# Eight small moves in the order of a three-block transformer kernel: taps, operands, banks, yields

## The chip, the cores and the metric

The kernel runs on one core of one Trainium2 chip. The metric is the device time of one execution in microseconds; less is better. Everything is fp32 at the edges.

## What is computed

Three residual blocks follow each other on one sequence of 1024 tokens of width 1024. Block 1 mixes an mLSTM branch (a causal convolution of width 4, gates, a chunkwise recurrence), a differential causal attention and a memory attention. Block 2 mixes a banded attention and a spatial gating unit and has a gated feed-forward part. Block 3 has 16 meta tokens, an LRU branch, a convolution branch of width 31 and a feed-forward part of width 4096. Between the blocks stand RMS norms. Cut to what matters here:

```python
def reference(x, mem, ...):
    x = first_block(x, mem, norm_g, w_in, conv_w, ...)
    x = second_block(x, norm_mix_2, w_in_2, ..., w_ffn_in_2, w_ffn_out_2, norm_final_2)
    return third_block(x, meta_tokens_3, norm_mix_g_3, w_in_3, ..., cc_conv_w_3, ..., norm_final_g_3)

def rmsnorm(x, g):
    return x * lax.rsqrt(jnp.mean(x * x, axis=-1, keepdims=True) + EPS) * g

# block 1, differential attention
pd = p[:, :, 0] - lam * p[:, :, 1]
outs.append(jnp.einsum('bhqk,bhkd->bhqd', pd, v[:, :, :hi]))
# block 2, feed-forward
g, up = jnp.split(hn @ w_ffn_in[l], 2, axis=-1)
h = h + (jax.nn.silu(g) * up) @ w_ffn_out[l]
# block 3, feed-forward
m = rmsnorm_3(h, norm_mlp_g[l]) @ w_mlp_up[l]
h = h + jnp.square(jax.nn.relu(m)) @ w_mlp_down[l]
```

## The kernel before

**Exact products from two halves.** TensorE multiplies fp32r operands. Every fp32 operand is split into a rounded high half and the rest: `split` (line 170) lets ACT cast the high half and DVE subtract it (line 175). `mm3` (lines 161 to 168) then makes three matmuls: high by high, high by low, low by high. Weights come by DMA on SP's queue (line 65) and are split whole by ACT (line 76) and DVE (line 77) into tiles `wsplit`; four of these rotate. A dense product is tiled into 128x512 output tiles, each 8 slices of the inner dimension by 3 matmuls.

**Banks.** PSUM is held as two banks `mm`, two score tiles `sc` of two banks each, and two tiles `tp` for transposes and sums. Where the order of work needs several outputs at once (the first product behind each norm), `gemm_fm` with `group=2` walks over the inner dimension for two outputs at a time and takes its banks from `banks` (line 147): two `mm`, then the four halves of the score tiles, and so on.

**The order of work.** The program is written as Python generators. A main stream issues products unit by unit, and `tick()` after each unit steps side generators (norms, attention steps, convolutions, loads), each up to its next `yield`. What is issued first comes first in a list scheduler, which then orders each engine's queue by it and by readiness. `high_priority` pulls the evictions of PSUM ahead, and `behind(...)` holds an instruction behind given others.

**Norms and seams.** At the end of a block the last product's eviction adds to the residual (L1341 in block 2, L1735 in block 3, L781 in block 1), ACT squares and POOL adds the squares (`square_sum`, L206). `norm_gen` (line 463) sums them by matmul, takes a reciprocal root on DVE in small steps (`rsqrt`, lines 189 to 194), broadcasts it by a transpose (`row_of`, L226), and makes eight split tiles `xs[k, h]` for each half h of the tokens. Where two norms follow each other (the seams 1 to 2 and 2 to 3) a second factor `fg` is multiplied in (line 485).

**Block products.** Two wide feed-forward products are made in `block_gemm` (line 366) with seven products of sums in place of eight: `block_tokens` (line 339) makes the token sums T1 to T4 by DVE and splits them; `operand(j)` (line 378) makes the weight sums `ssum` on POOL (L385, L386, L388, L390) and splits them. Six operands are made ahead of the matmul (L413). `block_up` (line 1435) makes the product of the first four weights while `block_tokens` runs at its side; then `block_gemm` starts and makes its first operands.

**Other places.** `mlstm_gen` (line 880): per channel tile four DVE steps of the convolution (L889, L891), then two tanh on ACT (L895); L702 is an ACT eviction of a unit beside it. `diff_out` (line 1180): for head and pair of query blocks, transposes, splits and value matmuls with a yield after each. `block3` starts with `conv_taps(0)` (line 1707): a DMA of the taps on POOL's queue, a cast on ACT (L1862) and a subtract on DVE. `conv_w` (line 1866) makes convolution matrices, one half on POOL, one on DVE (L1872), in the `wsplit` tiles of the weights; one matrix serves eight steps of three matmuls (L1890). `final` (line 1796): the last product in column pieces of 512 and 256, with the add on DVE (L1810), squares on ACT, sums on POOL (L206), and the sums' matmul (L214).

Of the kernel before, what the change touches and what calls it, by code (L numbers as in the profile page):

```python
# [95 lines left out]
class Kern:  # L96
# [4 lines left out]
    def __init__(self, tc, A):  # L101
        self.tc, self.nc, self.A = tc, tc.nc, A
        self.sides = []


# [41 lines left out]
    def banks(self):  # L147

        while True:
            yield self.mm()  # L150
            yield self.mm()
            for _ in (0, 1):
                sc = self.sc()
                yield sc[:, :512]
                yield sc[:, 512:]

    def tp(self):
# [71 lines left out]
    def gemm_fm(self, n_units, src, evict, halves=(0, 1), N=512, lag=1, gate=None, post=None, wait=None, ahead=True,  # L229
# [4 lines left out]
        if group:  # L234
# [5 lines left out]
            for h in halves:  # L240
                for g in range(0, lag, group):
# [9 lines left out]
                    for k in range(8):  # L251
# [6 lines left out]
                        if k % 2 or len(us) > 2:  # L258
                            yield
                    late += [(u, h, pss[u - g]) for u in us]  # L260
                    if group > 3 or post is not None or (h == halves[-1] and us[-1] == lag - 1):
                        with self.tc.high_priority(offset=PRIO_E):
                            ends()
# [102 lines left out]
    def block_gemm(self, n, B, page, out):  # L366
# [11 lines left out]
        def operand(j):  # L378
# [16 lines left out]
            return w, o  # L395
        ps, x12 = {}, {}
        for j, (p, i) in enumerate(seq):
            for q in range(len(ready), min(j + 6, len(seq))):
# [64 lines left out]
    def norm_gen(self, h, u, g, xs, acc, acc2=None, fg=None, r_d=None, lead=1, stay=False, tight=None):  # L463
# [19 lines left out]
        if fg is not None:  # L483
            gg = self.nsm.tile([128, 8], F32, name="ngg")
            nc.vector.tensor_mul(gg, fg, g)
        else:
            gg = g
# [392 lines left out]
    def mlstm_gen(self):  # L880
# [4 lines left out]
        for k in range(4):  # L885
            a = self.page(name="xcv")
            x = xm[k]
            cw = lambda t: v("conv_w", t * 4 + k)
            nc.vector.tensor_scalar(a, x, cw(3), v("conv_b", k), op0=OP.mult, op1=OP.add)  # L889
            for s in (1, 2, 3):  # L890
                nc.vector.scalar_tensor_tensor(a[:, s:], x[:, :1024 - s], cw(3 - s), a[:, s:], op0=OP.mult, op1=OP.add)  # L891
            for h in (0, 1):
                t = self.half_tmp("ct")
                s = slice(h * 512, h * 512 + 512)
                nc.scalar.activation(t, a[:, s], AF.Tanh)  # L895
                nc.vector.scalar_tensor_tensor(a[:, s], t, 1.0, a[:, s], op0=OP.add, op1=OP.mult)
            xcv.append(a)
            yield
# [281 lines left out]
    def diff_out(self, vd):  # L1180

        nc = self.nc
        for hd in range(4):
            od = self.xpage(name="od")
            for i in range(4):
# [4 lines left out]
                for c in range(i + 1):  # L1190
# [8 lines left out]
                    for k in (0, 1):  # L1199
# [3 lines left out]
                        self.mm3(acc[:, o:o + n], vd[hd, kt // 4], (kt % 4) * 128, 128, t, k * 256, n, kt == 0, last)  # L1203
                    if c < i:
                        yield
# [44 lines left out]
    def block2(self, xs, gens):  # L1250
# [148 lines left out]
        def out(i, block, t, ps):  # L1399
# [7 lines left out]
            else:  # L1407
                self.ends = nc.vector.tensor_mul(t, t, ps),
                store(2 + i, 0, t)
        self.block_up(uu, xs, gens, B, dict.fromkeys(("T1", "T2", "T3", "T4"), self.split_page), ev_up)  # L1410
        for _ in self.block_gemm(20, B, page, out):
            self.tick()
# [21 lines left out]

    def block_up(self, u, xs, gens, B, pages, ev):

        def blocks():
            while any(g in self.sides for g in gens):
                yield
            yield from self.block_tokens(u, xs, gens, B, pages)  # L1440
        tg = self.spawn(blocks())
        for _ in self.gemm_fm(4, lambda k, h: xs[k, h], ev, lag=4, wait=xs, ahead=False, group=2):
            self.tick()
        self.finish(tg, *gens)
# [160 lines left out]
    def block3(self, u2, xs, gens):  # L1605
# [100 lines left out]
        self.hl, self.co = {}, {}  # L1706
        self.conv_taps(0)
        self.spawn(self.conv_in())
# [12 lines left out]
        for i, q in enumerate(SEQ_3):  # L1721
            n = len(" ".join(SEQ_3[:i + 1]).split()) - u0
            for _ in self.gemm_fm(n, src, lambda u, h, ps: ev(u + u0, h, ps),
                                  post=lambda u: (lambda j, w: meta(j + u0, w)) if units[u + u0][0] != "l" else None):
                self.tick()
# [47 lines left out]
        xsp = lambda: self.xpage((128, 2, 512), F32R, "sp")  # L1773
        self.block_up(uu, xs, gens, B, dict(T1=self.split_page, T2=xsp, T3=xsp, T4=self.split_page), ev_up)
        first = [self.xpage, self.xpage]

        def page(shape=(128, 1024), name="pg"):
            return (first.pop() if first else self.page)(shape, F32, name)
        for _ in self.block_gemm(14, B, page, out):
            self.tick()  # L1780
# [15 lines left out]
    def final(self, u3, src):  # L1796
# [4 lines left out]
        for o, n in FINAL:  # L1801
            acc = self.page((128, n), name="acc")
            h, off = divmod(o, 512)
            for m in range(8):
# [4 lines left out]
                with self.tc.high_priority(offset=PRIO_E):  # L1809
                    nc.vector.tensor_add(u, u, ps[:, :n])  # L1810
                    self.square_sum(acc, u, m == 0, eng=nc.gpsimd)
                self.tick()
# [53 lines left out]
    def conv_w(self, i):  # L1866

        for j in range(i, min(i + 2, 9)):
            if j not in self.cw:
                w = self.cw[j] = self.ws.tile([128, 2, 1024], F32R, name="wsplit")  # L1870
                for a, eng in enumerate((self.nc.gpsimd, self.nc.vector)):
                    eng.tensor_tensor(w[:, a, :].rearrange("p (n c) -> p n c", c=32),  # L1872
                                      self.cmask[:, None, :].to_broadcast([128, 32, 32]),
                                      self.taps[a][:, j * 32:j * 32 + 32, None].to_broadcast([128, 32, 32]), op=OP.mult)
        return self.cw.pop(i)

# [344 lines left out]
```

## Time and profile before

| | us |
|---|---|
| median of 3 runs | 3361.07 (3359.77 to 3361.33) |
| the profiled execution's own time | 3369.31 |
| its span in the trace | 3367.6 |
| TensorE busy in the span | 3267.9 |
| VectorE, ScalarE, GpSimd busy | 1914.6, 1167.1, 473.1 |
| mean granted clock of TensorE | 0.987 |

The page counts an engine as busy while an instruction of it runs. A row of a timeline gives the start, the duration, engine and line, the tile written and the tiles read, the shape, how many instructions it stands for, and in brackets how long the engine was idle before it and what it waited for. A row of the windows gives a stretch's length, PE's busy time with its count of matmuls, the granted clock as a share of full speed, the busy share of the DMA engines and GB/s.

### The profile page before, as it was taken

The numbers are of one execution on the slowest core, as the hardware profiler recorded it, in microseconds if no ns is written. First come the engines' busy times: TensorE is split into PE (matmuls) and PEld (weight loads), VectorE is DVE, ScalarE is ACT, GpSimd is POOL, SyncE is SP. The second block draws the span as 40 slices with busy tenths as digits, with TensorE's granted clock in tenths as the row PEclk, the third lists the DMA queues.
The fourth block names the chain that finished last, engine by engine and source line by source line (L and its number), as shares of the span: only waits on it lengthen the run. The fifth ranks groups of instructions, "written<-read, shape, count | busy, mean of one in ns | idle before, by whom it ended". The sixth has DMA issues, their size and how long they took to land.

```text
span 3367.6 us, 41745 instructions
## 1 busy us (share of the span) xinstructions
PE 3267.9 (97%) x16039; PEld 2668.9 (79%) x16039; DVE 1914.6 (57%) x3627; ACT 1167.1 (35%) x2112; POOL 473.1 (14%) x445
## 2 busy tenths in 40 slices
PE   7999999999999999999999999999999999999998
PEld 5788877777777988887788887887878788888887
DVE  6555556665665554346755556445558865554444
ACT  4222344432454442213433333134453443332211
POOL 0000000001300000012223221031202222220002
PEclk9999999999999999999999999999999999999999
DMA  3323211221211144323122235122111333362211
GB/s 116 129 100 125 90 57 38 80 109 63 80 48 41 65 142 163 128 97 128 58 86 82 86 134 190 58 84 70 50 57 66 104 113 105 118 253 96 67 51 57
DMA packets 128632, 318.53 MB, mean 95 GB/s; under 512 B 16304, under 2 KB 34864, under 8 KB 128432
## 3 DMA queue, kind: packets, MB, share of 16 engines
q1 hardware_dynamic: 103392, 234.01, 20.3%
q0 software_dynamic: 21440, 76.51, 6.5%
q10 hardware_dynamic: 3600, 5.34, 0.5%
q8 instruction: 126, 2.06, 0.3%
q14 instruction: 74, 0.61, 0.1%
HBM read 232.90 MB, written 82.90 MB: 94 GB/s over the span
## 4 chain that ended last, share of the span: by engine, by line
PE 82%; DVE 8%; issue 5%; ACT 2%; DMA 2%; POOL 1%; ACTq 0%; POOLq 0%; DVEq 0%; SPq 0%
PE mm L166 16%; PE mm L167 16%; PE mm L168 16%; PE mm L413 10%; PE sc L413 8%; DVE sp L175 1%; PE mm L1890 1%; PE sc L1158 1%; PE sc L166 1%; PE sc L1468 1%; PE sc L167 1%; PE sc L168 1%; DVE wsplit L77 1%; PE tp L166 1%; PE tp L167 1%
## 5 line engine op out<-in xcount | busy, mean ns | idle before, releaser
L166 PE MATMUL mm<-sp,wsplit 128*128 128x512 f32 (+1 forms) x2720 | 1085.5, 400 | 19.1 <-DVE ur L1341 6.7
L167 PE MATMUL mm<-sp,wsplit 128*128 128x512 f32 (+1 forms) x2720 | 1068.5, 393 | 2.8 <-DVE sp L1983 2.5
L168 PE MATMUL mm<-sp,wsplit 128*128 128x512 f32 (+1 forms) x2720 | 1066.9, 392 | 0.0
L166 PEld LDWEIGHTS mm<-sp,wsplit 128*128 128x128 f32 x2720 | 516.9, 190 | 129.5 <-DVE ur L1341 7.8
L167 PEld LDWEIGHTS mm<-sp,wsplit 128*128 128x128 f32 x2720 | 517.4, 190 | 103.6 <-DVE sp L1983 4.1
L168 PEld LDWEIGHTS mm<-sp,wsplit 128*128 128x128 f32 x2720 | 516.5, 190 | 104.8 <-issue 0.8
L413 PE MATMUL mm<-sp,wsplit 128*128 128x512 f32 x1632 | 390.0, 391 | 3.9 <-ACT hd L1761 1.8
L76 ACT CAST wsplit<-wraw 128x1024 fp32r<-128x1024 f32 x196 | 205.5, 1049 | 509.8 <-PE mm L168 475.1
L413 PEld LDWEIGHTS mm<-sp,wsplit 128*128 128x128 f32 x1632 | 305.8, 188 | 71.1 <-DVE scp L430 2.4
L77 DVE TENSOR_TENSOR wsplit<-wraw,wsplit 128x1024 fp32r<-128x1024 f32 x196 | 248.0, 1267 | 164.4 <-ACT wsplit L76 162.8
L413 PE MATMUL sc<-sp,wsplit 128*128 128x512 f32 x1224 | 296.6, 391 | 3.8 <-ACT scp L419 3.0
L413 PEld LDWEIGHTS sc<-sp,wsplit 128*128 128x128 f32 x1224 | 230.6, 189 | 53.7 <-ACT scp L419 3.5
L206 POOL TENSOR_TENSOR acc<-acc,sqt 128x512 f32<-128x512 f32 (+1 forms) x105 | 135.5, 1303 | 471.2 <-ACT sqt L205 382.1
L1735 DVE TENSOR_TENSOR ur<-ur,mm 128x512 f32<-128x512 f32 x112 | 76.9, 686 | 145.3 <-PE mm L168 145.2
L175 DVE TENSOR_TENSOR wsplit<-ssum,wsplit 128x512 fp32r<-128x512 f32 x136 | 101.0, 743 | 93.4 <-ACT wsplit L175 93.3
L1341 DVE SCALAR_TENSOR_TENSOR ur<-mm,ur 128x512 f32<-128x512 f32 x96 | 66.2, 690 | 107.2 <-PE mm L168 107.1
L175 ACT CAST wsplit<-ssum 128x512 fp32r<-128x512 f32 x136 | 82.8, 621 | 108.9 <-POOL ssum L390 35.0
L388 POOL TENSOR_TENSOR ssum<-ssum,wraw 128x512 f32<-128x512 f32 x34 | 51.4, 1512 | 248.8 <-DVE wsplit L175 248.8
L175 ACT CAST wsplit<-wraw 128x512 fp32r<-128x512 f32 x102 | 61.8, 620 | 68.3 <-PE sc L413 47.6
L175 ACT CAST sp<-hraw 128x512 fp32r<-128x512 f32 x108 | 63.3, 620 | 51.9 <-PE mm L168 43.7
L166 PE MATMUL mm<-wsplit,sp 128*128 128x256 f32 x256 | 76.8, 300 | 1.8 <-ACT ot L702 1.8
L175 DVE TENSOR_TENSOR sp<-hraw,sp 128x512 fp32r<-128x512 f32 x108 | 71.1, 686 | 6.6 <-ACT sp L175 6.6
(567 smaller groups left out, 4440.0 us busy)
## 6 DMA issues: line engine op xcount, KB each, us to landing
wraw<-W SPq DMA_DIRECT2D x264, 512.0 KB, 3.7
hraw<-hid_d POOLq DMA_DIRECT2D x54, 512.0 KB, 5.0
hid_d<-scp SPq DMA_DIRECT2D x68, 256.0 KB, 2.0
t_d<-gl SPq DMA_DIRECT2D x32, 256.0 KB, 2.0
u<-x_d POOLq DMA_DIRECT2D x16, 512.0 KB, 6.3
gl<-t_d POOLq DMA_DIRECT2D x32, 256.0 KB, 3.1
u_d<-u SPq DMA_DIRECT2D x32, 256.0 KB, 2.0
ur<-u_d POOLq DMA_DIRECT2D x16, 512.0 KB, 9.3
```

Of the source, the lines that this page charges most:

```text
L76: K.nc.scalar.copy(s[:, 0, :], r)
L77: K.nc.vector.tensor_sub(s[:, 1, :], r, s[:, 0, :].bitcast(F32))
L166: t.matmul(ps, wh, xh, start=first, stop=False)
L167: t.matmul(ps, wh, xl, start=False, stop=False)
L168: t.matmul(ps, wl, xh, start=False, stop=last)
L175: return nc.scalar.copy(hi, src), nc.vector.tensor_sub(lo, src, hi.bitcast(F32))
L206: eng.tensor_add(acc, acc, t[:, :acc.shape[-1]])
L388: nc.gpsimd.tensor_sub(s, s, a11)
L413: nc.tensor.matmul(d, wk[:, c, :], xk[:, e, :], start=new and k == y == 0, stop=k == 3 and y == 2, skip_group_check=not new)
L1158: nc.tensor.matmul(pss[m][:, kb * 512:kb * 512 + w], qt[P, a, qs], kt[P, b, :w], start=i == 0, stop=i == 2 and not diag)
L1341: nc.vector.scalar_tensor_tensor(uu(m, h), ps, 0.5, uu(m, h), op0=OP.mult, op1=OP.add)
L1735: nc.vector.tensor_add(uu(m, h), uu(m, h), ps)
```

## The change

Eight places are edited. (1) `banks` gives the score halves first, then the `mm` banks. (2) `block_gemm` makes its first four operands in front of its loop, with a yield after each two; `block_up` steps it there after T1 and after T2, but not before three groups of its own product are issued. (3) `norm_gen` yields once more in the seams. (4) `mlstm_gen` yields between convolution and tanh. (5) `diff_out` leaves out the three yields of the last head's last pair. (6) the first `conv_taps` is held behind the last split of the norm that was issued. (7) the products of block 3 call `conv_ws(0, 2)` at their last unit, which makes the first two convolution matrices of the pass that follows. (8) `final` adds the squares of the 256-wide pieces on DVE in place of POOL.

```diff
     def banks(self):
         while True:
-            yield self.mm()
-            yield self.mm()
             for _ in (0, 1):
                 sc = self.sc()
                 yield sc[:, :512]
                 yield sc[:, 512:]
+            yield self.mm()
+            yield self.mm()
...
                     late += [(u, h, pss[u - g]) for u in us]
+                    self.groups += 1
...
         ps, x12 = {}, {}
+        for q in range(4):
+            ready[q] = operand(q)
+            if q % 2:
+                yield
         for j, (p, i) in enumerate(seq):
...
             nc.vector.tensor_mul(gg, fg, g)
+            yield
...
                 nc.vector.scalar_tensor_tensor(a[:, s:], x[:, :1024 - s], cw(3 - s), a[:, s:], op0=OP.mult, op1=OP.add)
+            yield
             for h in (0, 1):
...
-                    if c < i:
+                    if c < i and (hd < 3 or i < 3):
                         yield
...
-            yield from self.block_tokens(u, xs, gens, B, pages)
+            for i, _ in enumerate(self.block_tokens(u, xs, gens, B, pages)):
+                if i in (1, 3):
+                    while self.groups < 3:
+                        yield
+                    next(bg)
+                yield
+        self.groups = 0
...
-        self.conv_taps(0)
+        with self.behind(*self.cut):
+            self.conv_taps(0)
...
             for _ in self.gemm_fm(n, src, lambda u, h, ps: ev(u + u0, h, ps),
+                                  gate=lambda u: u < n - 1 or self.conv_ws(0, 2),
...
-                    self.square_sum(acc, u, m == 0, eng=nc.gpsimd)
+                    self.square_sum(acc, u, m == 0, eng=nc.gpsimd if n > 256 else None)
...
     def conv_w(self, i):
-        for j in range(i, min(i + 2, 9)):
+        self.conv_ws(i, min(i + 2, 9))
+        return self.cw.pop(i)
+
+    def conv_ws(self, a, b):
+        for j in range(a, b):
             if j not in self.cw:
...
-        return self.cw.pop(i)
+        return True
```

In blocks 2 and 3 the generator `bg = self.block_gemm(...)` is made before `block_up`, which gets it as an argument, and run to its end behind it.

## Rows read from the trace of the kernel before

**Rows 1.** The page's part 1: busy time, share and instructions of each engine.

```profile
PE 3267.9 (97%) x16039; PEld 2668.9 (79%) x16039; DVE 1914.6 (57%) x3627; ACT 1167.1 (35%) x2112; POOL 473.1 (14%) x445
```

**Rows 2.** PE's waits by releaser: us in total, times, longest.

```profile
PE mm L1890 <- DVE wsplit L1872: 4.9, 3, 3.0
```

**Rows 3.** Windows for PE: stretch, length, busy (matmuls), granted clock, DMA share, GB/s.

```profile
112.00:120.00 8.00, 6.16 (x41) 0.79 0.18 58
824.00:834.00 10.00, 8.50 (x25) 0.66 0.53 161
875.00:885.00 10.00, 9.23 (x37) 0.83 0.35 110
1646.00:1656.00 10.00, 8.72 (x32) 0.83 0.47 157
2042.00:2052.00 10.00, 6.44 (x20) 0.66 0.55 204
```

**Rows 4.** Timelines of ACT, DVE and PE behind 2042 us.

```profile
2042.27 0.43 ACT L1862 CAST ctaph<-ctap 128x288 fp32r<-128x288 f32 x1 [4.42 <-DMA ctap<-taps]
...
2043.60 0.62 ACT L175 CAST sp<-hraw 128x512 fp32r<-128x512 f32 x1
...
2043.68 1.23 DVE L77 TENSOR_TENSOR wsplit<-wraw,wsplit 128x1024 fp32r<-128x1024 f32 x1 [5.02 <-ACT wsplit L76]
...
2045.56 0.79 PE L166 MATMUL mm<-sp,wsplit 128*128 128x512 f32 x1 [4.90 <-DVE ur L1341]
```

**Rows 5.** Timeline of PE at the end of the diff attention.

```profile
822.12 1.06 PE L226 MATMUL tp<-ident,dv 128*128 128x128 f32 x8 [2.00 <-DVE dv L194]
...
825.50 0.79 PE L166 MATMUL mm<-sp,wsplit 128*128 128x512 f32 x1 [2.31 <-ACT sp L175]
```

**Rows 6.** Timelines of PE, POOL and ACT at the first blocks of block 2.

```profile
1637.33 3.02 PE L413 MATMUL mm<-sp,wsplit 128*128 128x512 f32 x12 [0.49 <-DVE silu L581]
...
1639.21 2.21 POOL L388 TENSOR_TENSOR ssum<-ssum,wraw 128x512 f32<-128x512 f32 x1 [40.71 <-DVE wsplit L175]
...
1645.61 1.14 ACT L175 CAST wsplit<-ssum 128x512 fp32r<-128x512 f32 x2 [3.05 <-POOL ssum L390]
...
1647.28 1.22 PE L413 MATMUL sc<-sp,wsplit 128*128 128x512 f32 x2 [3.05 <-ACT scp L419]
```

**Rows 7.** Timelines of PE, POOL and DVE in the seam from block 1 to 2.

```profile
875.76 0.79 PE L166 MATMUL mm<-sp,wsplit 128*128 128x512 f32 x1 [1.52 <-DVE u L781]
...
877.91 2.98 POOL L206 TENSOR_TENSOR acc<-acc,sqt 128x512 f32<-128x512 f32 x2 [1.41 <-ACT sqt L205]
...
879.67 2.31 DVE L77 TENSOR_TENSOR wsplit<-wraw,wsplit 128x1024 fp32r<-128x1024 f32 x1
```

**Rows 8.** Timeline of PE at three waits for a bank or an operand.

```profile
1592.96 0.50 PE L166 MATMUL mm<-sp,wsplit 128*128 128x512 f32 x1 [1.67 <-DVE u L1341]
...
2686.03 0.50 PE L166 MATMUL mm<-sp,wsplit 128*128 128x512 f32 x1 [1.68 <-DVE u L1735]
...
2731.67 1.65 PE L413 MATMUL mm<-sp,wsplit 128*128 128x512 f32 x6 [1.75 <-ACT hd L1761]
```

**Rows 9.** Timelines of ACT and PE beside the mLSTM's convolution.

```profile
112.89 1.15 ACT L895 ACTIVATE ct<-xcv 128x512 f32<-128x512 f32 x2 [0.82 <-DVE xcv L891]
...
114.36 0.45 PE L166 MATMUL mm<-wsplit,sp 128*128 128x256 f32 x1 [1.84 <-ACT ot L702]
```

**Rows 10.** POOL's convolution matrices (ns min/median/max, first and last start); PE's first convolution matmuls.

```profile
L1872 POOL TENSOR_TENSOR wsplit<-cmask,ctaph x18: 1914/2797/3892, 2352.7 to 2559.2; 128x1024 fp32r<-128x1024 f32 x18
...
2383.87 1.30 PE L1890 MATMUL mm<-chl,wsplit 128*128 128x256 f32 x9 [0.20 <-issue]
```

**Rows 11.** Timelines of DVE, POOL and PE at the tail.

```profile
3355.73 0.42 DVE L1810 TENSOR_TENSOR ur<-ur,mm 128x256 f32<-128x256 f32 x1 [0.17 <-PE mm L168]
...
3356.80 0.72 POOL L206 TENSOR_TENSOR acc<-acc,sqt 128x256 f32<-128x256 f32 x1 [0.64 <-ACT sqt L205]
...
3357.58 0.61 PE L214 MATMUL tp<-ones,acc 128*128 128x1 f32 x4 [1.89 <-POOL acc L206]
```

More of the change, by code (lines that the diff above doesn't have):

```diff
@@ L1409, in out @@
                 store(2 + i, 0, t)
-        self.block_up(uu, xs, gens, B, dict.fromkeys(("T1", "T2", "T3", "T4"), self.split_page), ev_up)
-        for _ in self.block_gemm(20, B, page, out):
+        bg = self.block_gemm(20, B, page, out)
+        self.block_up(uu, xs, gens, B, dict.fromkeys(("T1", "T2", "T3", "T4"), self.split_page), ev_up, bg)
+        for _ in bg:
             self.tick()
@@ L1433, in block2, with block_up @@
         return u2, r
-    def block_up(self, u, xs, gens, B, pages, ev):
+    def block_up(self, u, xs, gens, B, pages, ev, bg):
         def blocks():
@@ L1439, in blocks @@
                 yield
-            yield from self.block_tokens(u, xs, gens, B, pages)
+            for i, _ in enumerate(self.block_tokens(u, xs, gens, B, pages)):
[4 more added lines that the diff above has]
+                yield
+        self.groups = 0
         tg = self.spawn(blocks())
@@ L1773, in block3 @@
         xsp = lambda: self.xpage((128, 2, 512), F32R, "sp")
-        self.block_up(uu, xs, gens, B, dict(T1=self.split_page, T2=xsp, T3=xsp, T4=self.split_page), ev_up)
         first = [self.xpage, self.xpage]
@@ L1778, in page @@
             return (first.pop() if first else self.page)(shape, F32, name)
-        for _ in self.block_gemm(14, B, page, out):
+        bg = self.block_gemm(14, B, page, out)
+        self.block_up(uu, xs, gens, B, dict(T1=self.split_page, T2=xsp, T3=xsp, T4=self.split_page), ev_up, bg)
+        for _ in bg:
             self.tick()
@@ L1866, in conv_w @@
     def conv_w(self, i):
-        for j in range(i, min(i + 2, 9)):
+        self.conv_ws(i, min(i + 2, 9))
+        return self.cw.pop(i)
+    def conv_ws(self, a, b):
+        for j in range(a, b):
             if j not in self.cw:
                 w = self.cw[j] = self.ws.tile([128, 2, 1024], F32R, name="wsplit")
-                for a, eng in enumerate((self.nc.gpsimd, self.nc.vector)):
-                    eng.tensor_tensor(w[:, a, :].rearrange("p (n c) -> p n c", c=32),
+                for p, eng in enumerate((self.nc.gpsimd, self.nc.vector)):
+                    eng.tensor_tensor(w[:, p, :].rearrange("p (n c) -> p n c", c=32),
                                       self.cmask[:, None, :].to_broadcast([128, 32, 32]),
-                                      self.taps[a][:, j * 32:j * 32 + 32, None].to_broadcast([128, 32, 32]), op=OP.mult)
-        return self.cw.pop(i)
+                                      self.taps[p][:, j * 32:j * 32 + 32, None].to_broadcast([128, 32, 32]), op=OP.mult)
+        return True
     def conv_pair(self, ms):
```

## The prediction, made before the changed kernel ran

> **What bounds the kernel now.** I read the page's engine line first, then PE's waits by releaser, then the granted clock of stretches, then the timelines round the gaps that the edits name. TensorE is busy for 97% of the span [rows 1], and no edit takes a matmul away. So the change can only return two things: the idle time of PE, 3367.6 − 3267.9 = 99.7 us in the whole span, and the time that PE loses at the lower of its two clock levels behind some of the gaps. The busy share of the other engines says nothing here; what counts is, gap by gap, which wait ended last.
>
> The clock matters as much as the gaps. A gap of some 2 to 5 us is followed by a stretch in which the granted clock falls from 2.4 to 1.2 GHz for a part of it: 0.66 over the 10 us behind the diff attention's two gaps, 0.66 behind the largest gap, 0.83 in the two others and 0.79 in an 8 us stretch of the first block [rows 3]. Such a stretch costs (1 − clock) × its length: 3.4, 3.4, 1.7, 1.7 and 1.7 us. Where the gap closes I count this as returned too.
>
> **The sum, part by part** (against the profiled execution's 3369.31 us, span and 1.7 us around it; it is 8.2 us above the median of the runs).
>
> *Tap cast behind the norm.* ACT idles 4.42 us for the taps' DMA and casts at 2042.27; the weight cast behind it in ACT's order, then DVE's subtract (which waited 5.02), then the eviction that frees PE's bank all shift with it, and PE stands 4.90 us until 2045.56 [rows 4]. Gap and clock: 4.90 + 3.4 = 8.3. Held behind the norm's last split, the tap cast leaves this chain, and the weight cast can go early. The tap DMA stays where it is on POOL's queue, so the page of hidden units issued behind it lands no sooner: its cast still starts at 2043.60 [rows 4], its DVE half stands ahead of the second eviction, and PE, after one unit of some 2.7 us (12 matmuls took 3.02 with the drain of the last [rows 6]), finds its second bank late by about 2 us. I take 4.9 − 2.0 + 3.4 = 6.3, less 0.8 for an imperfect clock: **−5.5** (ends: 0 if the hidden page merely takes the taps' place, −8.3). The cast itself, 0.43 us on ACT, lands some 240 us later beside norm work that DVE bounds; cost nothing, 0.4 without that cover.
>
> *Diff attention without its last three yields.* The last head's end has too few GEMM units beside it: PE waits 2.00 for DVE's reciprocal chain and 2.31 for ACT's split [rows 5], and pays 3.4 in clock: 7.7 together. Three yields fewer start these chains three units, 3 × 2.7 = 8.2 us, sooner, more than both gaps. The matmuls come in denser order, so PE can meet an unfinished split among them: I keep 1.2 for that, **−6.5** (ends +1, −7.7).
>
> *First operands of the block GEMM.* In block 2 POOL's L388 sat idle 40.71 us until a DVE split, and the four POOL sums that follow reach ACT at 1645.61 only; ACT's eviction stands behind that cast, and PE waits 3.05 [rows 6] (the wait is put down to the eviction, but ACT itself had idled for POOL). Another 0.49 sits before the first block matmuls. With 1.7 of clock: 5.2. Made between the token sums, the four operands are ready well before the first block matmul. Each such POOL sum lies beside DVE subtractions, so I keep 1.0: **−4.2** (ends +4.4, see below, and −5.2).
>
> *The gaps at banks.* At 1592.96 PE waits 1.67 for the eviction that frees a bank, at 2686.03 1.68, and at 2731.67 1.75 in block 3's operand step [rows 8]. Score banks first and the operands ahead give PE four more banks before it must wait: 5.1, less 1.0, for the token splits arrive hardly sooner: **−4.1** (0 to −5.1). In the second block's attention the first score tiles now find score banks not yet evicted: not shown before, between 0 and the 3.05 that PE waited for one [rows 6]; I take **+1**, nearer 0, as four of six banks are free by then.
>
> *The two seams.* In the seam from block 1 to 2 PE waits 1.52 at 875.76, with 1.7 of clock. But DVE works there without a break: the weight subtract at 879.67 takes 2.31, until 881.98 [rows 7]; only then comes the last split of the half, and PE can't finish its first group before that, whatever bank it has. A bank ahead moves PE's gap from one place to another. The second seam repeats the pattern. Norm broadcast one tick later: nothing, as it stands behind the same DVE. Together **−1.0** (+2 to −6.5).
>
> *The extra yield between convolution and tanh in block 1.* ACT takes two tanh at 112.89, ahead of the eviction PE waits 1.84 for [rows 9]; with 1.7 of clock, 3.5. The tanh now comes a unit later, when DVE's convolution is done. Four ticks more fit beside the GEMM. **−2.8** (0 to −3.5), since the tanh can meet the next eviction instead.
>
> *Convolution matrices ahead.* PE waits 4.9 us in 3 gaps for them [rows 2]. But POOL's first matrix is already made at 2352.7, while the first matmul that uses one comes at 2383.87 [rows 10]: the order of readiness does this without the edit. Later matrices cost POOL 2.8 each, PE uses one in about 3.0 (24 matmuls, nine of which took 1.30), so the rest of the pass runs at POOL's pace as before. **0** (−4.9 to +5).
>
> *Tail.* The last sum is 0.72 on POOL; DVE adds an equal piece in 0.42 [rows 11]. −0.3 of the 1.89 gap, and a little for DVE no longer running beside POOL: **−0.6**. DVE takes 8 × 0.42 = 3.4 us more per piece; if it falls behind PE there, +2.
>
> Sum: −5.5 − 6.5 − 4.2 − 4.1 + 1 − 1.0 − 2.8 + 0 − 0.6 = −23.7. The profiled execution would come to 3345.6, the median from 3361.07 to 3337.4.
>
> **POOL against DVE.** In the seam the weight subtract on DVE took 2.31 us while POOL's sums ran (two in 2.98 from 877.91), against 1.23 for the same tile with POOL quiet [rows 4, 7]: 1.1 lost for a POOL sum. Four POOL sums put among the token subtractions could so take 4 × 1.1 = 4.4 us from DVE where DVE makes the operands PE waits for, in each of two blocks: 8.8. The Trainium skill, "SBUF — State Buffer", "Who interferes with whom", has such a rule: a DVE instruction with two SBUF inputs and a GpSimd instruction that reads SBUF exclude each other for the whole instruction. By that rule the operands' gain would be gone; the rows agree with the sign and with the size of one collision.
>
> **The rivals.**
> (a) *The sum holds*: 3337, chance 0.52; own range 3330 to 3345.
> (b) *Only tap cast and diff attention pay*, since they alone take a wait away; elsewhere PE waits for the next producer in DVE's or ACT's order. −5.5 − 6.5 = −12: 3349. For it: the DVE queue of the seams without a break [rows 7]; against it: ACT's and POOL's idle time in [rows 6]. Chance 0.19.
> (c) *POOL holds DVE at the operands*: −23.7 + 8.8 = −15: 3346. For it the 2.31; against it that the sums are spread over the whole token stage. Chance 0.08.
> (d) *Everything pays in full*, the seams (−6.5) and the convolution (−4.9) too and no part kept: −8.3 − 7.7 − 5.2 − 5.1 − 6.5 − 3.5 − 4.9 − 0.6 = −42, or −37 with the hidden page's 2 and the +1 and the tail's doubt: 3324. Chance 0.09.
> (e) *It does not do what it says*: the scheduler orders by readiness, as with the first matrices [rows 10], and the new places in the program alter little. −3: 3358. Against it: ACT's waiting tap cast shows that an early place in the program does bind an engine. Chance 0.06.
> (f) *Slower by starved matrices.* The split buffers number four; the two matrices made before the last weight is fetched take two. If weights hold the other two through the convolution pass, production runs in series with use: 2.7 us for each of the 14 later matrices of two passes = +38, net +14: 3375. It decides at the second held buffer; by the code one weight is held there, so three rotate. Chance 0.06.
>
> **How the numbers follow.** A measurement of this kernel tells about 0.2%, 6.7 us, from no change; faster means under 3354.3, slower over 3367.8. Cases (a) and (d), nearly all of (c) and most of (b) lie under: 0.85. (e) and the rest of (b): 0.09. (f): 0.06. The range 3325 to 3352 takes in (a), (b) and (c) with their bounds and stops at the edge of (d).
>
> **What would show it.** Right: no gap over 2.5 us for the eviction behind the taps' cast, and that cast behind the last split of the norm; no waits over 1 us for the reciprocal and the split at the end of diff attention, and the clock at 1.0 there; the POOL sums of the first operands tens of us ahead of the first block matmul; no tanh directly ahead of the eviction in the first block. DVE in the seams is to stay without a break. Wrong: a new low-clock stretch next to a new gap in the convolution passes, weight or operand subtracts of 2 us and more between the token sums, or a gap that has only moved with the total of PE's idle time near 100 us.

## The result, and the profile after

The changed kernel took 3341.94 us (median of 4 runs, 3340.15 to 3343.93) against 3361.20 (4 runs, 3359.77 to 3362.31): ratio 0.9943, interval 0.9931 to 0.9954. That is 19.3 us, or 0.57%, faster. The forecast was 3337 with a range of 3325 to 3352.

The profiled execution took 3340.15 us with a span of 3338.4, 1.8 us under its median, while the one before had lain 8.2 us above its own. The two traces therefore differ by 29.2 us, and some 10 us of that are not the change's. By the stages below, 4.5 of them lie between 735 and 790 us, where nothing was edited; and against its second profile the kernel before lost 2.3 us more at the taps and 1.7 us more in the seam from block 1 to 2. Part 1 of the changed kernel's page:

```profile
PE 3253.4 (97%) x16039; PEld 2660.1 (80%) x16039; DVE 1915.4 (57%) x3641; ACT 1168.2 (35%) x2112; POOL 465.7 (14%) x431
```

and the second to fourth of PE's waits by releaser (us in total, times, longest):

```profile
PE tp L227 <- DVE nr L195: 9.4, 5, 3.6
PE mm L1913 <- DVE wsplit L1895: 7.3, 3, 3.6
PE mm L167 <- ACT sp L176: 3.8, 2, 2.3
```

The work of PE is the same [rows 1], 16039 matmuls. Its idle time fell by 3367.6 − 3267.9 − (3338.4 − 3253.4) = 14.7 us, and the other 14.5 are shorter matmuls, that is, fewer of them at the lower clock (the mean granted clock rose from 0.987 to 0.992). The wait for the convolution matrices [rows 2] did not shrink: 7.3 us where 4.9 stood.

Since both orders hold the same matmuls, the time between the same two places of PE's order can be compared stage by stage. Lengths in us (starts are those of the changed kernel's trace). "Before" has three profiles: the one of the prediction, a second one of the same kernel, and the kernel before with the tap cast alone moved, whose lengths differ from the others' by the edit only at the taps (in brackets).

| stage, what was edited | before | changed | part undone |
|---|---|---|---|
| 84 to 126, mLSTM yield | 46.2, 45.8, 46.4 | 41.7 | 47.0 |
| 735 to 790, nothing | 60.2, 58.7, 60.2 | 55.7 | |
| 790 to 844, diff attention | 57.0, 56.5, 57.0 | 54.1 | 56.9 |
| 844 to 914, seam 1 to 2, first attention steps | 67.9, 66.2, 67.8 | 69.8 | banks 66.5 |
| 1570 to 1628, product beside the token sums | 60.0, 60.0, 60.1 | 57.7 | banks 61.0 |
| 1628 to 1983, block product of block 2 | 360.1, 360.2, 360.2 | 355.0 | operands 357.8 |
| 1983 to 2033, taps | 55.0, 52.7, (50.2) | 50.1 | 51.9 |
| 2238 to 2352, seam 2 to 3, meta tokens | 120.1, 120.1, 120.2 | 114.1 | banks 121.4 |
| 2352 to 2397, first convolution pass | 39.9, 39.9, 40.0 | 45.2 | banks 42.8, banks and gate 39.9 |
| 2654 to 2712, the same product in block 3 | 60.1, 60.1, 60.0 | 57.3 | banks 59.2 |
| 3292 to the end, tail | 47.6, 47.6, 47.6 | 46.8 | 47.8 |

The rows don't all repeat alike. Profiles that have the edit in question agree within 0.2 us for the diff attention and for block 2's two feed-forward stages. The mLSTM's stage lasts 39.3 to 42.3 us in the ten profiles with its yield, and the taps' stage 49.6 to 51.5 where the cast is moved. Between 126 and 400 us the mLSTM's yield changes PE's order itself; over 84 to 400 us, where both orders hold the same matmuls again, 319.3 to 319.9 us became 313.5 to 316.6, and with the yield undone it is 320.4. Eight of the edited stages gained, two lost: the first attention steps of block 2 and the first convolution pass.

### The profile page after: what moved, and what is told of

The parts are those of the page before. It is cut to its first block, busy times and chain, and to the rows that moved or that the text cites. A ratio compares the mean times of both kernels' runs of the same rounds, so it can differ in the third digit from the quotient of the medians.

```text
span 3338.4 us, 41731 instructions
## 1 busy us (share of the span) xinstructions
PE 3253.4 (97%) x16039; PEld 2660.1 (80%) x16039; DVE 1915.4 (57%) x3641; ACT 1168.2 (35%) x2112; POOL 465.7 (14%) x431
## 4 chain that ended last, share of the span: by engine, by line
PE 85%; DVE 6%; issue 4%; ACT 2%; DMA 1%; POOL 1%; ACTq 0%; DVEq 0%; POOLq 0%
PE mm L167 17%; PE mm L168 16%; PE mm L169 16%; PE mm L419 11%; PE sc L419 8%; PE sc L167 1%; PE sc L168 1%; PE sc L169 1%; PE mm L1913 1%; PE sc L1484 1%; PE sc L1166 1%; PE tp L167 1%; PE tp L168 1%; DVE sp L176 1%; PE tp L1503 1%
## 5 line engine op out<-in xcount | busy, mean ns | idle before, releaser
L167 PE MATMUL mm<-sp,wsplit 128*128 128x512 f32 (+1 forms) x2640 | 1048.2, 398 | 8.9 <-ACT sp L176 3.8
L168 PE MATMUL mm<-sp,wsplit 128*128 128x512 f32 (+1 forms) x2640 | 1032.3, 391 | 3.6 <-DVE sp L2006 2.4
L169 PE MATMUL mm<-sp,wsplit 128*128 128x512 f32 (+1 forms) x2640 | 1030.9, 390 | 0.0
L167 PEld LDWEIGHTS mm<-sp,wsplit 128*128 128x128 f32 x2640 | 498.2, 189 | 112.9 <-ACT sp L176 7.3
L168 PEld LDWEIGHTS mm<-sp,wsplit 128*128 128x128 f32 x2640 | 498.9, 189 | 101.4 <-DVE sp L2006 4.1
L169 PEld LDWEIGHTS mm<-sp,wsplit 128*128 128x128 f32 x2640 | 498.4, 189 | 101.0 <-issue 1.1
L419 PEld LDWEIGHTS mm<-sp,wsplit 128*128 128x128 f32 x1632 | 306.0, 188 | 69.0 <-DVE scp L436 2.4
L419 PE MATMUL sc<-sp,wsplit 128*128 128x512 f32 x1224 | 295.0, 390 | 1.3 <-DVE c L433 0.9
L207 POOL TENSOR_TENSOR acc<-acc,sqt 128x512 f32<-128x512 f32 x91 | 125.8, 1396 | 449.5 <-ACT sqt L206 360.2
L1349 DVE SCALAR_TENSOR_TENSOR ur<-mm,ur 128x512 f32<-128x512 f32 x96 | 66.2, 690 | 105.3 <-PE mm L169 105.1
L168 PE MATMUL sc<-sp,wsplit 128*128 128x512 f32 x240 | 96.3, 401 | 3.3 <-DVE sp L176 3.2
L167 PE MATMUL sc<-sp,wsplit 128*128 128x512 f32 x240 | 96.9, 404 | 1.5 <-ACT sp L176 1.5
L169 PE MATMUL sc<-sp,wsplit 128*128 128x512 f32 x240 | 95.3, 397 | 0.0
L176 ACT CAST wsplit<-wraw 128x512 fp32r<-128x512 f32 x102 | 61.8, 621 | 69.7 <-PE sc L419 47.6
```

What stands on the lines that cost most here:

```text
L167: t.matmul(ps, wh, xh, start=first, stop=False)
L168: t.matmul(ps, wh, xl, start=False, stop=False)
L169: t.matmul(ps, wl, xh, start=False, stop=last)
L176: return nc.scalar.copy(hi, src), nc.vector.tensor_sub(lo, src, hi.bitcast(F32))
L207: eng.tensor_add(acc, acc, t[:, :acc.shape[-1]])
L419: nc.tensor.matmul(d, wk[:, c, :], xk[:, e, :], start=new and k == y == 0, stop=k == 3 and y == 2, skip_group_check=not new)
```

## Experiments

Each edit is one to the changed kernel unless it says otherwise. By run times alone the banks undone (experiment 4), the banks in turn (5), the four moves (8) and the two (9) stand clear of the changed kernel, with no run in its range; the other parts undone differ from it by 1 to 4 us with runs that overlap, and what they are worth is read from the stages.

**1. The tap cast.** Undone:

```diff
-        with self.behind(*self.cut):
-            self.conv_taps(0)
+        self.conv_taps(0)
```

> The changed kernel with the tap cast where it was, ahead of the norm. Theory: PE's gap of about 4.9 us behind the tap cast comes back with its clock: 3346 to 3350, and the profile shows ACT idle over 3 us for the taps' DMA ahead of a weight cast. Rival: with the block product's operands made early the queues stand otherwise, the DMA has landed in time or the gap is under 1.5 us: 3341 to 3343.

3345.37 us, ratio to before 0.9956 (0.9943 to 0.9969): 0.13% above the changed kernel, with intervals that overlap. Its trace, ACT and PE:

```profile
2024.45 0.43 ACT L1880 CAST ctaph<-ctap 128x288 fp32r<-128x288 f32 x1 [1.36 <-DMA ctap<-taps]
...
2027.74 0.50 PE L167 MATMUL mm<-sp,wsplit 128*128 128x512 f32 x1 [2.16 <-DVE ur L1349]
```

The same chain as in [rows 4], but ACT waits 1.36 for the taps, not 4.42; PE's gap is 2.16, and no low clock follows (1.00 over the 10 us from 2026). That is neither the gap of 4.9 that was expected nor the rival's of under 1.5. The stage is 1.8 us longer than in the changed kernel's profile, and 0.3 longer than the longest of the profiles with the edit. The other way round, the kernel before with this one part added:

> The kernel before with the tap cast alone held behind the norm's last split. Putting the cast back into the changed kernel brought back a gap of 2.16 us and no low clock there. Theory A: the cast is worth what the prediction said where the taps' DMA lands late: the gap of 4.90 us goes down to 1 or less and the low clock (3.4 us) with it, 3355 to 3357. Theory B: it is worth 2 us only (the landing of that DMA differs from one execution to the next), and the rest of the 4.9 us that the stage gained came from other edits: 3359 to 3361, with a gap of 2 us or more for the eviction left there, or no low clock with the gap gone.

3358.95 us, ratio 0.9995 (0.9986 to 1.0004): not told from no change. In its trace PE's gap is gone:

```profile
2037.16 0.47 PE L166 MATMUL mm<-sp,wsplit 128*128 128x512 f32 x1 [0.85 <-DVE ur L1341]
```

and the stage is 50.2, 4.8 us less than in the profile of the prediction, but that profile was not the usual one. A second profile of the kernel before:

> The kernel before once more, for a second profile of it. Theory: the profile that the prediction rests on had a low-clock stretch or a gap more than the median execution (it lies 8.2 us above it); the gap behind the taps' DMA is between 2 and 5 us, since that DMA's landing is not the same in every execution. Rival: 4.90 us again and the same low-clock stretches at 677, 756, 824 and 2043 us, so that the 8 us lie elsewhere.

3361.49 us, close to the median. ACT and PE:

```profile
2034.89 0.43 ACT L1862 CAST ctaph<-ctap 128x288 fp32r<-128x288 f32 x1 [2.19 <-DMA ctap<-taps]
...
2038.18 0.50 PE L166 MATMUL mm<-sp,wsplit 128*128 128x512 f32 x1 [2.55 <-DVE ur L1341]
```

The taps' DMA took 5.0 us from issue to landing here; the gap is 2.55 with 1.7 us of clock behind it. So the cast was worth 1.8 (in the changed kernel) to 4.8 us by its stage, 2.5 where the time was near the median; the forecast rested on the late landing. Over the fourteen profiles that DMA took 4.7 to 6.9 us, and 6.9 is the one that the forecast was made from. In the changed kernel the weight cast goes ahead, as foretold, and the taps are in no one's way:

```profile
2020.44 0.47 PE L167 MATMUL mm<-sp,wsplit 128*128 128x512 f32 x1 [0.94 <-DVE ur L1349]
...
2022.14 1.05 ACT L76 CAST wsplit<-wraw 128x1024 fp32r<-128x1024 f32 x1
```

**2. The yields of diff attention.**

```diff
-                    if c < i and (hd < 3 or i < 3):
+                    if c < i:
```

> The changed kernel with the three yields of the last diff attention step put back. Theory: the yields paid for the reciprocal's gap (2.00 us) and half of the clock (1.7), while the gap of 2.31 for the split stays with and without them: 3345 to 3347. Rival, the prediction's term: 6.5, so 3348 to 3350. Rival: nothing, as the last probabilities set the end of the step: 3341 to 3343.

3345.79 us, ratio 0.9958 (0.9944 to 0.9972). PE at the end of the step, with the yields:

```profile
816.45 1.06 PE L227 MATMUL tp<-ident,dv 128*128 128x128 f32 x8 [2.00 <-DVE dv L195]
819.83 0.80 PE L167 MATMUL mm<-sp,wsplit 128*128 128x512 f32 x1 [2.31 <-ACT sp L176]
```

and without them, the changed kernel:

```profile
810.37 1.03 PE L227 MATMUL tp<-ident,dv 128*128 128x128 f32 x8
813.72 0.73 PE L167 MATMUL mm<-sp,wsplit 128*128 128x512 f32 x2 [2.31 <-ACT sp L176]
```

The first gap goes, the second stays to the hundredth. PE's order is the same in both: the broadcast L227 is the last thing in it that does not need this head's split tiles. An earlier end moves the broadcast and what follows it alike, and what lies behind it is one chain through DVE and ACT. The stage takes 56.9 against 54.1: 2.8 us, a little under what this run was expected to show and far from the 6.5 of the prediction.

**3. The gate for the convolution matrices.** The line `gate=lambda u: ...` taken out:

> The changed kernel without the gate in the products of block 3 (the first two convolution matrices are made when the convolution pass asks for them). Theory of the prediction: the scheduler makes them ahead anyway, so nothing changes within 2 us: 3340 to 3344, gaps for matrices (L1895) 7 us or so in sum as with the gate. Rival 1: the gate is what brought the 4.9 us gained between 2300 and 2380 us: 3345 to 3348, with a gap before the first convolution matmul. Rival 2: the gate makes the pass worse, since it holds two of four buffers through the last unit: 3336 to 3339, and the gap of 3.58 us in the first pass goes back to about 1.7.

3343.17 us, ratio 0.9945 (0.9932 to 0.9958): no difference, as forecast. Its gap in the first pass is 3.58 too. That left the question what had made the pass 4 to 5 us longer. With banks and gate both undone:

> The changed kernel with both the gate (part 7) and the bank order (part 1) undone, for its first convolution pass. With either one undone PE's gap there stays at 3.58 to 3.63 us, and DVE takes the recurrence's 4 us step 12.9 to 16.5 us behind the first convolution matmul, against 11.0 in the kernel before. Theory: each of the two edits by itself moves the matrices ahead of the recurrence's steps on DVE, so with both undone the step is at 11.0 again and the gap at 1.7. Rival: a third edit does it (the tap cast behind the norm, or the operands), and the gap stays at 3.6.

One execution, 3341.52 us. (That it is no slower than the changed kernel says nothing of the banks: it is one of the two profiles in which the stage 735 to 790 is 4.5 us shorter than in most.) DVE and PE of it:

```profile
2369.16 3.89 DVE L2057 TENSOR_TENSOR_SCAN xc<-la,lmx,lb 128x1024 f32<-128x1024 f32 x1
2372.97 5.72 DVE L1894 TENSOR_TENSOR wsplit<-cmask,ctap 128x1024 fp32r<-128x1024 f32 x2
...
2375.89 1.32 PE L1912 MATMUL mm<-chl,wsplit 128*128 128x256 f32 x9 [1.69 <-DVE wsplit L1894]
```

and of the changed kernel:

```profile
2369.40 2.94 DVE L1895 TENSOR_TENSOR wsplit<-cmask,ctap 128x1024 fp32r<-128x1024 f32 x1
2372.26 4.00 DVE L2058 TENSOR_TENSOR_SCAN xc<-la,lmx,lb 128x1024 f32<-128x1024 f32 x1
2376.18 5.13 DVE L1895 TENSOR_TENSOR wsplit<-cmask,ctap 128x1024 fp32r<-128x1024 f32 x3
...
2379.10 1.23 PE L1913 MATMUL mm<-chl,wsplit 128*128 128x256 f32 x4 [3.58 <-DVE wsplit L1895]
```

PE waits for the matrix half that DVE makes behind the recurrence's scan. In the kernel before, and with both edits undone, the scan starts 11.0 us behind the pass's first matmul; in the changed kernel 16.5, and PE runs dry at another matrix. With the gate alone undone it is 16.5 as well, with the banks alone undone 12.9, and the gap stays at 3.58 and 3.63. So each of the two edits is enough to delay the scan, and undoing one alone does not show it; undoing both gives 39.9 us and the gap of 1.69. How either edit comes to put matrices ahead of the scan was not followed further. The clock behind the gap (0.71 over the 10 us from 2374 in the changed kernel, 1.00 in the other) is in those lengths.

**4. The banks, part 1 undone** (mm banks first again in `banks`).

> The changed kernel with mm banks first again (part 1 undone), operands early. Theory: the score banks first gain 1.5 to 2 us each in the second product of block 2, the same in block 3, 3.4 in the seam from block 1 to 2 and 4.9 behind the seam from 2 to 3, and lose 5.3 at the first attention of block 2; so undoing it costs 1.7 + 1.7 + 3.4 + 4.9 - 5.3 = 6.4: 3346 to 3350, the gap at the first attention gone. Rival: with DVE bound in the seams the two cancel: 3341 to 3344.

3349.59 us, ratio 0.9963 (0.9950 to 0.9975), 7.7 us over the changed kernel. The bank waits are back:

```profile
1583.55 0.50 PE L167 MATMUL mm<-sp,wsplit 128*128 128x512 f32 x1 [1.68 <-DVE u L1349]
...
1629.78 0.97 PE L419 MATMUL mm<-sp,wsplit 128*128 128x512 f32 x3 [1.45 <-DVE silu L588]
```

and the first attention steps are quick again. By stages: +3.3, +1.9, +7.3 (seam 2 to 3 and meta tokens), −2.4 (convolution), −3.2 (seam 1 to 2 with attention). It is the largest part of the change, and it holds one of the two losses.

**5. That loss.** In the changed kernel, PE:

```profile
896.80 0.55 PE L1484 MATMUL sc<-sp 64*128 64x128 f32 x3
898.35 0.55 PE L1484 MATMUL sc<-sp 64*128 64x128 f32 x3 [1.00 <-DVE ast L1487]
900.68 1.27 PE L1484 MATMUL sc<-sp 64*128 64x256 f32 x6 [1.79 <-DVE ast L1489]
901.88 0.79 PE L167 MATMUL mm<-sp,wsplit 128*128 128x512 f32 x1
```

Block 2's first product has four groups. With score banks first, the third takes the mm banks and the fourth a score tile, and ahead of the fourth stand the two first attention steps, which want both score tiles each. They pass through DVE one after the other while PE waits. The edit gives score and mm banks in turn there:

```diff
                 yield sc[:, :512]
                 yield sc[:, 512:]
+                if mixed:
+                    yield self.mm()
+                    yield self.mm()
```

> The changed kernel (3341.9 us), with the first product of block 2 alone taking its banks as score, mm, score, mm. Theory: with score banks in the fourth group, the first two attention steps hold both score tiles until DVE and ACT have read them, and PE loses 2.8 us in two gaps and 3.4 us at the lower clock there. The gaps of 1.00 and 1.79 us at L1484 go, and the time falls by 3 to 6 us, to 3336 to 3339. Rival: the mm banks of the fourth group then keep the next unit waiting for their evictions, or the gap only moves: 3341 to 3344, with a gap of over 1 us in the 20 us behind.

3334.63 us, ratio 0.9925 (0.9912 to 0.9938), 7 us under the changed kernel. Windows for PE, changed kernel, then this one (length, busy, granted clock, DMA share, GB/s):

```profile
896.00:910.00 14.00, 11.21 (x46) 0.76 0.23 75
```

```profile
896.00:910.00 14.00, 14.00 (x71) 1.00 0.26 80
```

Both gaps and the low clock are gone, and the stage falls from 69.8 to 65.1, under the 66.2 to 67.9 of before. The time fell more than was expected.

**6. The operands, part 2 undone** (no operands ahead of the loop, no `next(bg)`).

> The changed kernel without the early operands (part 2), banks and all else as changed. Theory: the operands alone close PE's gap of 3.05 us for the score bank of block 2 and its 1.7 us of clock, and the 1.75 at the start of block 3's blocks: 5 to 6.5 us back, 3347 to 3349. Rival: the bank order has closed them (P1 finds a free mm bank), so 3341 to 3344 and no gap over 1 us at L413 of the kernel before. Rival: POOL's sums among the token subtractions cost DVE time, so it gets faster by 2 or more in the 60 us in front: 3338 to 3340.

3345.39 us, ratio 0.9960 (0.9947 to 0.9972). PE at the score bank:

```profile
1640.35 0.94 PE L415 MATMUL sc<-sp,wsplit 128*128 128x512 f32 x3 [1.65 <-DVE scp L423]
```

The operands are worth 2.8 us in block 2's stage and 0.9 to 2.3 in block 3's (58.2 against 57.3 in the changed kernel's profile and 55.9 in others of this series). By run times it cost 3.5 us to undo them, where 5 to 6.5 was expected. Part 1 takes from the same wait: with the banks undone and the operands early (experiment 4) the 3.05 us of [rows 6] are gone as well and the stage 1628 to 1983 has the changed kernel's length, while the banks without the operands leave the 1.65. The two parts undone alone cost 3.3 + 2.8 = 6.1 us in the two stages, of the 7.4 that both together gained. The POOL sums did spread over the token stage, as the changed kernel's row for the fourth operand shows, 44.9 us behind the start of its stage, where [rows 6] has it 59.3 behind:

```profile
1615.17 1.67 POOL L390 TENSOR_TENSOR ssum<-ssum,wraw 128x512 f32<-128x512 f32 x1 [26.33 <-DVE wsplit L176]
```

It starts 10 us ahead of the block product's first matmul, at 1624.90. Beside it DVE's token sums are stretched (two that take 1.28 us with POOL quiet):

```profile
1615.01 2.38 DVE L357 TENSOR_TENSOR u<-u,u 128x512 f32<-128x512 f32 x2
```

Yet the stage in which they lie is hardly longer with them: 57.7 against 57.5.

**7. Three small parts undone**: the mLSTM yield, the norm's yield, the tail's adds.

> The changed kernel with three parts undone: the mLSTM yield (4), the norm's yield in the seams (3) and the tail's adds on DVE (8). They lie in stages of their own, so the trace tells them apart. Theory: the mLSTM yield is worth 4.5 us at 108 to 126 us (gap of 1.84 or more for the eviction L702 of before and 1.7 to 3.4 of clock come back), the tail 0.8, and the norm's yield costs rather than gains (+1 without DVE cover in the seams), so its undoing gives 0 to 2 back: 3345 to 3347 in sum. Rival: the mLSTM gap is small without the yield too, as in other executions: 3341 to 3343.

3344.96 us, ratio 0.9948 (0.9935 to 0.9962). By stages: mLSTM +5.3, the two seams −0.5 each, tail +0.9. ACT and PE beside the mLSTM:

```profile
124.98 1.15 ACT L901 ACTIVATE ct<-xcv 128x512 f32<-128x512 f32 x2 [4.29 <-DVE xcv L897]
126.04 0.37 ACT L708 ACTIVATE ot<-mm 128x256 f32<-128x256 f32 x1
...
126.46 0.38 PE L167 MATMUL mm<-wsplit,sp 128*128 128x256 f32 x1 [1.03 <-ACT ot L708]
```

The picture of [rows 9], one unit later: two tanh ahead of the eviction. With the yield a pair of tanh still stands directly ahead of an eviction at 119.21, but PE does not wait for that one. The norm's yield gains nothing: without it PE waits 1.46 us at the broadcast of each seam and not behind it.

**8. Four moves more.** The banks of 5; the end of diff attention begun without its yield; `high_priority` round the convolution matrices and round the last norm's reciprocal.

> The changed kernel with four more moves: score and mm banks in turn in the first product of block 2 (measured: 4.6 us in its stage); the last head's end of diff attention started without its yield, so two units earlier; the convolution matrices, and the last norm's reciprocal, at the priority of evictions. Expected from the stages: 4.6; 2.31 + 1.7 of clock where PE waits for the last split of diff attention; 3 of the 3.58 + 3.06 us that PE waits for the DVE half of a matrix that stands behind the recurrence's 4.00 us step on DVE, and 1.7 to 3.4 of clock; 1.1 at the end, where the reciprocal stands behind scalings: 3341.9 - 4.6 - 4 - 5 - 1.1 = 3327. Rival: matrices wait for a free buffer, not for DVE, so priority gives nothing or moves the wait to the recurrence, and the end of diff attention only meets the next wait: 3333 to 3336.

3351.44 us, ratio 0.9972 (0.9960 to 0.9984): slower than the changed kernel. The banks' 4.6 us are there, but the diff stage is 9.3 us longer, with these rows of PE and ACT:

```profile
815.47 0.80 PE L171 MATMUL mm<-sp,wsplit 128*128 128x512 f32 x1 [4.51 <-ACT sp L180]
...
823.98 0.79 PE L171 MATMUL mm<-sp,wsplit 128*128 128x512 f32 x1 [5.21 <-ACT sp L180]
...
823.31 1.14 ACT L180 CAST sp<-yraw 128x512 fp32r<-128x512 f32 x2 [7.38 <-DMA yraw<-yd_d]
```

In the second gap PE waits for a page of this branch that comes back from DRAM. In the changed kernel POOL issues the two loads of this kind at 739.1 and 746.2; here the second stands in POOL's queue behind two loads that wait 71.67 us:

```profile
816.17 1.05 POOL L1300 DMA_DIRECT2D bias<-bias  x2 [71.67 <-DVE sp L180]
817.22 0.53 POOL L796 DMA_DIRECT2D yraw<-yd_d  x1
```

In experiment 9, without the earlier end and without the matrices' priority, that load is issued at 747.1 again. So one of those two moves put late loads ahead of one that PE needs soon; most likely it was the earlier end, but they were not tried apart. The priority left the matrices of the first pass where they were (scan at 16.5, gap 3.58), and the second pass got longer, 44.9 us from its first matmul to its last against 40.1. Of the other three moves only the reciprocal's priority gave something: 0.4 us of the 1.1 expected.

**9. The two moves that paid**, the banks of 5 and the reciprocal's priority:

> The changed kernel with score and mm banks in turn in the first product of block 2 (3334.6 us measured) and the last norm's reciprocal at the priority of evictions (0.4 us less in the stage of the tail): 3332 to 3336. Rival: the 4.6 us of the banks' stage are lost again to the clock elsewhere: 3338 to 3342.

3336.51 us, ratio 0.9923 (0.9911 to 0.9936): with experiment 5 the fastest, and not told from it.

## Why the forecast was right, and what in it was not

The time lies in the range, 5 us from the point, and the sign and most mechanisms held: gaps that the edits name closed, and PE's idle time and its time at the lower clock fell. The sum held better than its terms, though: tap cast and diff attention gave less than was said, the second seam and the bank waits more, and two stages lost. That these misses nearly cancelled is luck.

*The price of the clock.* (1 − clock) × length counts the lower level also while PE still stands in the gap, which the sum has already. At the taps [rows 3, 4] these are the windows of PE in which it idles until 2045.56:

```profile
2042.00:2044.00 2.00, 0.00 (x0) 0.77 0.98 373
2044.00:2046.00 2.00, 0.44 (x1) 0.50 0.95 344
```

Of the 3.4 us, 0.23 × 2.00 + 0.50 × 1.56 = 1.2 lie inside the 4.90, so gap and clock came to 7.1 there and not 8.3.

*Tap cast* (−5.5): mechanism as described; the size was that of one late landing. It measured 1.8 to 4.8, and 2.5 in the profile near the median. No gap over 0.94 us is left for that eviction.

*Diff attention* (−6.5): mis-sized. The step from three units sooner to "more than both gaps" took the two gaps for separate lateness. Only the 2.00 went; the 2.31 hangs on the broadcast and moves with it, and the clock behind it is 0.83 over 10 us where 1.00 was foretold. Measured −2.8.

*Operands* (−4.2) and *gaps at banks* (−4.1): the stages 1570 to 1983 and 2654 to 2712 gave 2.3 + 5.2 + 2.8 = 10.3 together. The sum was 2 too small. The collision of POOL's sums with DVE (rival c) did come, 1.1 us in the row of experiment 6, but the stage got no longer by it. It was also smaller than four sums for each block: by the code the first four operands hold three, and in block 2 POOL had made two of them early in the kernel before as well, the second in the first of these rows:

```profile
1596.87 1.64 POOL L386 TENSOR_TENSOR ssum<-wraw,wraw 128x512 f32<-128x512 f32 x1 [1.80 <-DMA wraw<-W]
1639.21 2.21 POOL L388 TENSOR_TENSOR ssum<-ssum,wraw 128x512 f32<-128x512 f32 x1 [40.71 <-DVE wsplit L175]
```

*Score banks in block 2* (+1): the mechanism was named, the price was not. I took four of six banks as free; the attention steps want two whole score tiles, and their turn comes before the fourth group's. Measured +4.7 (69.8 against 65.1), most of it two gaps of 2.8 and the clock behind them.

*Seams* (−1.0): the step "A bank ahead moves PE's gap from one place to another", with DVE working without a break as its reason, failed. The changed kernel's DVE and PE in the first seam:

```profile
851.21 0.75 DVE L503 SCALAR_TENSOR_TENSOR nt<-u,ngg,tp 128x512 f32<-128x512 f32 x1 [0.59 <-POOL acc L207]
...
861.88 0.75 DVE L503 SCALAR_TENSOR_TENSOR nt<-u,ngg,tp 128x512 f32<-128x512 f32 x1 [1.19 <-POOL acc L207]
...
863.88 0.50 PE L168 MATMUL sc<-sp,wsplit 128*128 128x512 f32 x1 [1.22 <-DVE sp L176]
```

DVE now has breaks, and PE still ends its group sooner: the sums of the second half (L215) start 19.9 us behind the first broadcast, at 868.89 against 849.03, where 22.8 lay between them before (884.50 and 861.70; 21.2 in the second profile). The breaks are not what gains: with the banks alone undone DVE has them too, and PE waits 1.70 and 1.95 us there; with the norm's yield undone DVE has none, and those waits stay away. The first seam gained 1.1 to 2.8 us apart from the attention (65.1 with the banks in turn against 66.2 to 67.9). The second gained 6.0 together with the meta tokens' product, which the prediction did not count at all; without the bank order it is +1.3 against before.

*Convolution* (0): right that the gate does nothing by itself, wrong for the stage. The bound of +5 was stated without a mechanism, and the only one named for a loss here, in rival (f), was buffers; what came was the recurrence's scan in DVE's queue, 4 to 5 us. With it came a sign that the prediction gave for being wrong, a new gap with low clock next to it in a convolution pass. Rival (f), starved buffers through both passes, is refuted: the gaps round the second pass sum to what they were (8.7 us in 69.1 against 8.9 in 69.9).

*Rival (b)*, that only tap cast and diff attention pay, is refuted by experiment 4, where undoing the banks alone costs 7.7, and by the 2.8 us of stage in experiment 6.

*mLSTM yield* (−2.8, −3.5 at most): 45.8 to 46.4 became 39.3 to 42.3, and over the longer stretch to 400 us it is 3 to 6 us. Later gaps of the same kind that I had not listed went with the first, such as the one of 1.03 in experiment 7. *Tail* (−0.6): −0.8. The last sum comes 0.2 sooner, but the reciprocal behind it is 1.1 later:

```profile
3327.23 2.04 DVE L1852 SCALAR_TENSOR_TENSOR ur<-ur,vec,tp 128x256 f32<-128x256 f32 x5
3329.19 0.15 DVE L1845 TENSOR_SCALAR nv<-tp 128x2 f32<-128x2 f32 x1
...
3331.66 0.66 PE L227 MATMUL tp<-ident,nr 128*128 128x128 f32 x2 [3.62 <-DVE nr L195]
```

DVE, given the adds, is still scaling the piece before. The gain of the tail is in its two gaps of 0.8 before that.

## What to carry to other kernels

A gap is worth its length only where the next thing in that engine's order is ready; look up what the engine does behind the gap, and whether a later gap hangs on the same chain. Giving one stage other banks or buffers gives the next stage other ones too: here the same edit gained in three stages (7.3, 3.3 and 1.9 us by experiment 4) and lost 4.7 in another, and taking banks in turn there won that back. Low clock that falls inside a gap is not a second price. And one profile is one execution: where a wait ends on a DMA, take a second profile before its length goes into a sum.

## What the runs showed of the hardware

The same gap of PE is not followed by the same clock. At 748 us in the changed kernel, and at the same place of PE's order in the others, PE waits 1.72 or 1.73 us for the same releaser in all fourteen profiles. By (1 − clock) × length 5.1 us are then lost to the lower clock in eleven of them, 3.4 in one and nothing in two. Windows of 14 us for PE from about the same place: the kernel before in the profile of the prediction,

```profile
753.00:767.00 14.00, 12.28 (x29) 0.63 0.09 32
```

its second profile,

```profile
753.00:767.00 14.00, 13.61 (x42) 0.76 0.01 2
```

and the changed kernel:

```profile
747.00:761.00 14.00, 12.28 (x52) 1.00 0.12 39
```

No edit is there. What decides between them the runs do not show. By the stage table it is 4.5 of the 10 us by which the two profiles differ more than the medians.

One DVE instruction has two lengths. The matrix half on DVE, nine times in the first pass of the changed kernel (ns min, median, max):

```profile
L1895 DVE TENSOR_TENSOR wsplit<-cmask,ctap x9: 1210/1226/2941, 2319.0 to 2380.1; 128x1024 fp32r<-128x1024 f32 x9
```

Which of the two it is goes by who starts first. DVE and POOL in the changed kernel:

```profile
2359.68 1.23 DVE L1895 TENSOR_TENSOR wsplit<-cmask,ctap 128x1024 fp32r<-128x1024 f32 x1 [1.51 <-PE mm L1913]
2359.71 2.97 POOL L1895 TENSOR_TENSOR wsplit<-cmask,ctaph 128x1024 fp32r<-128x1024 f32 x1 [0.79 <-PE mm L1913]
...
2363.68 2.93 DVE L1895 TENSOR_TENSOR wsplit<-cmask,ctap 128x1024 fp32r<-128x1024 f32 x1
```

The first DVE half starts 0.03 us ahead of POOL's and takes 1.23, and POOL's takes 2.97, where one with DVE quiet takes 1.91. The DVE half at 2363.68 starts while a POOL half runs, and takes 2.93. The Trainium skill, "SBUF — State Buffer", "Who interferes with whom", gives the rule: a DVE instruction with two inputs in SBUF and a GpSimd instruction that reads SBUF exclude each other. The rows agree. The recurrence's scan has two lengths as well, 2.35 us with POOL quiet and 4.00 beside POOL's halves in the rows of experiment 3:

```profile
2333.66 2.35 DVE L2058 TENSOR_TENSOR_SCAN xc<-la,lmx,lb 128x1024 f32<-128x1024 f32 x1
```

Whether a matrix made by one engine alone would come sooner was not tried.
